# Gated DeltaNet on one core: the last chunk's four heads stacked on the partitions, and 32-row diagonal blocks inverted by substitution without merge products

## The chip, the core and the metric

The kernel runs on one core of a Trainium2 chip. The core has a matrix engine (TensorE, PE in the profile; its weight loads are a row of their own, PEld), a vector engine (DVE), a scalar engine (ACT), GpSimd (POOL), and SyncE (SP), whose queue issues all DMA transfers of this kernel. Each engine has its own instruction stream, and they meet through semaphores. The metric is the device time of one execution in microseconds (us), smaller being better; it is given as the median of several runs.

## The reference, cut

The whole is a decoder trunk of two layers: a gated DeltaNet layer with its MLP, then a differential-attention layer with its MLP, model width 2048, 256 tokens and 16 meta tokens ahead of them, all in float32. The change is in the first layer only. There, for each of 32 value heads (16 heads of queries and keys, each used by two value heads, head width 128), a chunked recurrence is computed:

```python
def step(S, xs):
    qc, kc, vc, bc, gc = xs
    G = jnp.cumsum(gc, axis=-1)
    decay = jnp.exp(jnp.where(tri_incl, G[..., :, None] - G[..., None, :], -jnp.inf))
    kb = kc * bc[..., None]
    a_kk = jnp.where(tri_strict, jnp.einsum('bhik,bhjk->bhij', kb, kc) * decay, 0.0)
    rhs = jnp.concatenate([vc * bc[..., None], kb * jnp.exp(G)[..., None]], axis=-1)
    sol = lax.linalg.triangular_solve(a_kk, rhs, left_side=True, lower=True, unit_diagonal=True)
    u, w = sol[..., :DV], sol[..., DV:]
    v_new = u - jnp.einsum('bhik,bhkv->bhiv', w, S)
    a_qk = jnp.einsum('bhik,bhjk->bhij', qc, kc) * decay
    o = (jnp.einsum('bhik,bhkv->bhiv', qc * jnp.exp(G)[..., None], S)
         + jnp.einsum('bhij,bhjv->bhiv', a_qk, v_new))
    S = (S * jnp.exp(g_last)[..., None]
         + jnp.einsum('bhik,bhiv->bhkv', kc * jnp.exp(g_last - G)[..., None], v_new))
    return S, o
```

What matters is the unit lower triangular system of each chunk and head, and the state `S` that goes from chunk to chunk. Around it stand the input projections (`w_in`: queries, keys, values, an output gate, and the decay and beta logits), a causal convolution of four taps with SiLU, the norms of q and k, and the output projection `w_out`.

## The kernel before, in words

Activations stand with the features on the partitions, 272 tokens in the free dimension. Every large product (`mm3`, lines 147 to 157) runs three times in the type F32R: weights and activations are split into a high part and a rest, and high x high, rest x high and high x rest are summed (lines 152, 155, 156). For this, weights come as 1 MB tiles (`wraw`, three buffers, one DMA each), ACT writes the high part `whi` (line 137), DVE the rest `wlo` (line 139), in halves of 1024 columns. A tile's 16 k-steps are 48 matmuls.

The DeltaNet layer (`gdn`) cuts the 272 tokens into chunks of 128, 128 and 16, and the 32 heads into eight blocks of four. For each block b, in the program's main line: `keys(b)` (four projections for two heads of q and k), `values(b)` (four), `gates(b)` (four), and `gate_out(b - 2)`, the output products of the block before the last (sixteen column tiles of four k-steps). That is 256 k-steps a block. In `gates` and `gate_out` DVE also writes `oT` (line 792) and adds to `acc` (line 1000).

Beside the main line run generators: norms of q and k (`stats`), the score products and decays (`products`), the inverse (`solve`), and the recurrence (`core`). A small planner, `Flow`, decides where their instructions stand in the program. Each k-step of `mm3` advances its clock by 3 x 272 / 2400 = 0.34 units; a generator's `yield x` puts its next piece x units later; `flow.until` runs pieces, with no projection between them, until a condition holds. The scheduler that then orders each engine's instructions need not keep program order: it puts an instruction that is ready ahead of one that is not, and weight splits have high priority.

The steps that the change touches, for a block:

- `stats`: per head and operand, three transposes on PE (`ps_kn`, line 649, one for each chunk) and squares on ACT.
- `products`: per chunk, scores `ps_u` (line 706), decays on ACT (line 710), and `UA` on DVE (line 712), which holds minus the scaled triangle and the query scores. For the first two chunks the diagonal 16-row blocks are copied to DRAM (`scr`, sixteen DMAs, line 718); `below` (POOL) then clears the block diagonal of `UA`. The 16-token chunk is handled head by head on 16 partitions.
- `solve`: all 68 blocks of 16 x 16 (2 chunks x 4 heads x 8, and 4 of the last chunk) are read back as one block per partition (`na`), and `forward` inverts them by substitution, 15 steps of one multiplication (line 630) and one reduction (line 631) each. The inverses go through DRAM into `DT` (block diagonal, 128 x 128 for each chunk and head; lines 751 to 757) and `DT3`. `DT` has one buffer: the next block's solve is written only once the last product that reads it is (`free`).
- `core`: `merge(c)` makes 32-row diagonal inverses from pairs of 16-row ones: a DVE transpose (line 836), a product `ps_e` (line 840), an ACT copy, a product `ps_d` (line 846), an addition and a transpose on DVE (lines 848, 850), then `ps_n` (line 854), from which the chunk's remaining system is applied in three products `ps_a` (line 896) and finished by `ps_w` (line 916). `ps_s` (line 929) updates the state, `ps_o` (line 941) gives the output, `ps_ks` and `ps_qs` (line 880) are the state's part for the next chunk. For the 16-token chunk `ps_w`, `ps_o`, the transposes `ps_ot` (line 810), and the DVE and ACT steps between (lines 884, 947, 951, 966) are issued once for each of the four heads.

A float32 product outside `mm3` is two PE instructions, a transpose one. The planner's waits that the text uses: `SOLVE` 40 units after `solve`, `STEP` 3 units between steps of `core`, 35 and 2 for the last block. The values of block b + 1 (`turned` in `values`) wait for the second chunk of block b (`chunk` = 2), and the main line waits for them by

```python
flow.until(lambda: g["values"] >= hv - 1)
```

Of the kernel before, what the change touches and what calls it, by code (L numbers as in the profile page):

```python
# [21 lines left out]
NM = 16  # L22
SEQ = 256
# [7 lines left out]
G1 = 9  # L31
GB = 4
HOLD = 1
# [469 lines left out]
def gdn(ctx, tc, a, e):  # L503
# [21 lines left out]
    gt = ctx.enter_context(tc.tile_pool(name="gt", bufs=2))  # L525
    gk = ctx.enter_context(tc.tile_pool(name="gk", bufs=4))
# [15 lines left out]
    def decays(ps):  # L542
# [29 lines left out]
        nc.vector.reciprocal(bt, bt)  # L572
        yield GATES[1]
# [10 lines left out]
        nc.sync.dma_start(g_dram, rows)  # L584
        G, GL = gnat[:, 0], gnat[:, 1]
# [5 lines left out]
        nc.scalar.activation(eLast, eLast, AF.Exp)  # L591
        gated.append(True)

    g_dram = dram.tile([32, L], F32, name="g_dram", bufs=1)
# [9 lines left out]
    DT3 = gc.tile([NM, HB, NM], F32, name="DT3")  # L604
    KQ3 = gc.tile([P, 2, 64], F32, name="KQ3")
# [18 lines left out]
    def forward(na, xt):  # L624

        parts, w, n = xt.shape
        tmp = gt.tile([parts, w, n], F32, tag="fw_t", name="fw_t", bufs=1)
        for i in range(1, n):
            b = na[:, None, 0:i + 1, i].broadcast_to([parts, w, i + 1])
            nc.vector.tensor_tensor(tmp[:, :, 0:i + 1], xt[:, :, 0:i + 1], b, ALU.mult)  # L630
            nc.vector.tensor_reduce(xt[:, :, i], tmp[:, :, 0:i + 1], AX.X, ALU.add)
# [4 lines left out]
    def keys(b):  # L636
# [3 lines left out]
        st = gt.tile([P, 2, 3, 2], F32, tag="st", name="st")  # L640
        nc.vector.memset(st, 1.0)
# [3 lines left out]
        def stats(h, t):  # L645
            yield SLACKST
            pk = psk.tile([P, 512], F32, tag="k", name="ps_kn")
            for c, (o, n) in enumerate(CH):
                nc.tensor.transpose(pk[:n, c * P:(c + 1) * P], kq[:, h, t, o:o + n], ident)
            if t == 0:  # L650
                nc.scalar.copy(kn[:, :, h, :], pk[:, :256].rearrange("p (c d) -> p c d", d=P))
            for c, (o, n) in enumerate(CH):
                sq = gt.tile([P, P], F32, tag="dec", name="sqk", bufs=2)
                nc.scalar.activation(sq[:n], pk[:n, c * P:(c + 1) * P], AF.Square, accum_out=st[:n, t, c, h:h + 1])
            if (h, t) == (1, 0):
                yield from products(b, g, st)
# [8 lines left out]
    def products(b, g, st):  # L665
        kq, prev = g["kq"], g["prev"]
        while not gated or prev and not prev["laid"]:
            yield 1.0
        nc.vector.tensor_scalar(st, st, 4 * EPS, None, ALU.add)
        rs = rsqrt(st.rearrange("p t c h -> p (t c h)"), "rsg", [P, 12]).rearrange("p (t c h) -> p t c h", t=2, h=2)  # L670
        rq = g["rq"] = gk.tile([P, 3, 2, 2], F32, tag="sc_rq", name="sc_rq", bufs=2)
        negc = gk.tile([P, 3, 2, 2], F32, tag="sc_nc", name="sc_nc", bufs=2)
        sup = g["sup"] = gk.tile([P, 3, 2, 2], F32, tag="sc_sup", name="sc_sup", bufs=2)
        nk = g["nk"] = gk.tile([P, 3, 2], F32, tag="sc_nk", name="sc_nk", bufs=2)
        r2 = gt.tile([P, 3, 2], F32, tag="r2", name="r2")
        nc.vector.reciprocal(r2, st[:, 0])
        r2b = r2[:, :, :, None].broadcast_to([P, 3, 2, 2])
        nc.vector.tensor_tensor(sup, heads(beta, b), r2b, ALU.mult)
        nc.vector.tensor_scalar(negc, sup, -1.0, None, ALU.mult)

        nc.vector.scalar_tensor_tensor(nk, st[:, 0], 0.5, rs[:, 0], ALU.mult, ALU.mult)
        nc.vector.tensor_tensor(sup, sup, heads(eLast, b), ALU.mult)
        nc.vector.tensor_scalar(rq, rs[:, 1, :, :, None].broadcast_to([P, 3, 2, 2]), P ** -0.5, None, ALU.mult)
# [6 lines left out]
        nc.gpsimd.affine_select(gb[:NM, :, 256:L], gb[:NM, :, 256:L], pattern=[[0, HB], [1, NM]], base=0,  # L690
                                channel_multiplier=-1, compare_op=ALU.is_ge, fill=NEG)
        scr = dram.tile([2, HB, 8, NM, NM], F32, name="scr")
        scr3 = dram.tile([HB, NM, NM], F32, name="scr3")
        UA = g["UA"] = []
        for c, (o, n) in enumerate(CH):
            while prev and prev["chunk"] < min(c, 1):
                yield 1.0
            if c < 2:
                ua = gk.tile([P, HB, 2, P], F32, tag="UA", name="UA", bufs=3)
            else:  # L700
                ua = gk.tile([NM, HB, 2, NM], F32, tag="UA3", name="UA3", bufs=2)
            UA.append(ua)
            for h in range(2):
# [3 lines left out]
                for r in range(2):  # L707
# [4 lines left out]
                    nc.vector.scalar_tensor_tensor(ua[:, hv], pu_v, negc[:n, c, h, r:r + 1],  # L712
                                                   dec[:n, None, :n].broadcast_to([n, 2, n]), ALU.mult, ALU.mult)
                yield UGAP
            if c < 2:
                for bl in range(8):
                    q = slice(NM * bl, NM * bl + NM)
                    nc.sync.dma_start(scr[c, :, bl].rearrange("h j i -> j h i"), ua[q, :, 0, q])
                below(ua, NM)
            else:  # L720
                nc.sync.dma_start(scr3.rearrange("h j i -> j h i"), ua[:, :, 0, :])
# [3 lines left out]
        solve(scr, scr3)  # L725
# [11 lines left out]
    def solve(scr, scr3):  # L737

        nb = 2 * HB * 8
        na = gt.tile([nb + HB, NM, NM], F32, tag="na", name="na", bufs=1)  # L740
        xt = gt.tile([nb + HB, NM, NM], F32, tag="xt", name="xt", bufs=1)
        diag = lambda t: t.rearrange("p j i -> p (j i)")[:, 0:NM * NM:NM + 1]
        nc.gpsimd.memset(xt, 0.0)
        nc.gpsimd.memset(diag(xt), 1.0)
# [4 lines left out]
        scr2 = dram.tile([nb, NM, NM], F32, name="scr2")  # L749
        scr4 = dram.tile([HB, NM, NM], F32, name="scr4")  # L750
        nc.sync.dma_start(scr2, xt[:nb])
        nc.sync.dma_start(scr4, xt[nb:])
        for bl in range(8):
            q = slice(NM * bl, NM * bl + NM)
            nc.sync.dma_start(DT[q, :, :, q].rearrange("p c h j -> p (c h) j"),
                              scr2.rearrange("(x b) m j -> b m x j", b=8)[bl])
        nc.sync.dma_start(DT3, scr4.rearrange("h m j -> m h j"))

    def values(b, g):
# [3 lines left out]
        def turned(hv, vt):  # L763
# [3 lines left out]
            if not nv:  # L767
                nv.extend(gk.tile([P, HB, P], F32, tag="nv", name="nv", bufs=4) for _ in CH)
            pv = psk.tile([P, 512], F32, tag="k", name="ps_v")
            for c, (o, n) in enumerate(CH):  # L770
                nc.tensor.transpose(pv[:n, c * P:(c + 1) * P], vt[:, o:o + n], ident)
            for c, (o, n) in enumerate(CH):
                nc.scalar.activation(nv[c][:n, hv], pv[:n, c * P:(c + 1) * P], AF.Copy,
                                     scale=g["nk"][:n, c, hv // 2:hv // 2 + 1])
            g["values"] += 1

        for hv in range(HB):
# [4 lines left out]
            conv_silu(ps, m, vt)  # L782
            flow.add(turned(hv, vt))
# [11 lines left out]
    def core(b, g):  # L795
# [7 lines left out]
        def turned(c, o, n, ov):  # L803
# [5 lines left out]
            for hv in range(HB):  # L809
                nc.tensor.transpose(pT[:, hv * n:(hv + 1) * n], ov[:n, hv], ident[:n, :n])  # L810
# [9 lines left out]
        ms = gt.tile([P, len(CH), HB], F32, tag="o_ms", name="o_ms")  # L820
# [6 lines left out]
        def merge(c):  # L827

            us = work("us")
            nc.gpsimd.affine_select(us.rearrange("p h (b i) -> p h b i", i=32),  # L830
                                    UA[c][:, :, 0, :].rearrange("p h (b i) -> p h b i", i=32),
                                    pattern=[[0, HB], [-32, 4], [0, 32]], base=0, channel_multiplier=1,
                                    compare_op=ALU.is_ge, fill=0.0)
            below(UA[c], 32)
            e16 = work("e16")
            nc.vector.transpose(flat(e16), flat(DT[:, c]))
            yield step
            _, pE = bank("ps_e")
            for hv in range(HB):
                nc.tensor.matmul(pE[:, hv], us[:, hv], e16[:, hv], start=True, stop=True)  # L840
            ae = work("ae")
            nc.scalar.copy(ae, pE)
            yield step
            _, pD = bank("ps_d")
            for hv in range(HB):
                nc.tensor.matmul(pD[:, hv], ae[:, hv], DT[:, c, hv], start=True, stop=True)
            d32 = work("d32")
            nc.vector.tensor_tensor(d32, DT[:, c], pD, ALU.add)
            dn = work("dn")
            nc.vector.transpose(flat(dn), flat(d32))  # L850
# [6 lines left out]
            merged[c] = d32, NT  # L857
# [5 lines left out]
        for c, (o, n) in enumerate(CH):  # L863
            if c == 0:
                R = nv[0]
            else:
                left = lambda h, t: kq[:, h, t, o:o + n]
                pS, pSv = bank("ps_ks")
                if c < 2:
                    pQ, pQv = bank("ps_qs")  # L870
                    banks = ((pS[:n], 0), (pQ[:n], 1))
                else:

                    nc.scalar.copy(KQ3.rearrange("p h (t i) -> p h t i", i=32)[:, :, :, 0:n], kq[:, :, :, o:o + n])
                    left = lambda h, t: KQ3[:, h, 0:32 + n]
                    banks = ((pS[:32 + n], 0),)
                    pQv = pSv[32:]
# [400 lines left out]
```

## Time and profile before

| | |
|---|---|
| median of 3 runs | 3023.15 us (3022.2 to 3023.69) |
| the profiled execution: its own time | 3024.88 us |
| its span, first to last instruction | 3023.1 us |
| mean granted TensorE clock | 0.993 |
| DeltaNet layer in the span | about 0 to 1045 us |
| DeltaNet blocks with the full load | 125 us each (for example 383 to 508 us) |

The profile is of one execution. Times of windows count from the start of the span. A line of a group reads: source line, engine, operation, output <- inputs by the program's tile names, shapes, count | busy us, mean ns of one | idle time of the engine before them and what ended it. A line of a timeline reads: start, duration, the same name, and in brackets the idle time before and its releaser. Matmuls are pipelined, so their durations overlap, and their starts are to be read. A line of windows reads: window, its length, busy us and count of PE, PEld, DVE, ACT and POOL, granted clock, DMA share, GB/s; by one tile it has only the engine of that tile. A line of waits reads: who waited <- for whom: us in total, times, longest.

### The profile page before, as it was taken

What the parts mean: (1) busy time and instruction counts of PE and PEld (TensorE: products, weight loads), DVE (VectorE), ACT (ScalarE), POOL (GpSimd) and SP (SyncE); (2) the same over time, 40 slices, a digit from 0 to 9 for tenths busy, and PEclk for the clock granted to TensorE, in tenths of its full rate; (3) what the DMA queues carried; (4) which work ended last, traced back from release to release, by engine and by line L of the source; (5) the groups of instructions that cost most, each with busy time, mean ns of one, the idle gap of its engine ahead of it and who ended that gap; (6) DMA issues with size and microseconds to landing.
All of it is one profiled execution on the core that took longest, in us unless ns stands there. A gap on an engine that the chain in (4) does not pass through costs nothing. (4 is left out here: it accounts for less than half of the span.)

```text
span 3023.1 us, 57162 instructions
## 1 busy us (share of the span) xinstructions
PE 2981.0 (99%) x23747; PEld 2924.3 (97%) x23747; DVE 1943.6 (64%) x3452; ACT 1490.1 (49%) x2735; POOL 205.2 (7%) x208
## 2 busy tenths in 40 slices
PE   8999999999999899999999999999999999999998
PEld 8999999999999799999999999999999999999998
DVE  7777576776867674555555558777757555555555
ACT  4565555465555454444344434455555444444443
POOL 0100010000100220000000004300004000000001
PEclk9999999999999899999999999999999999999999
DMA  5433343434434444454544443433354555555553
GB/s 211 151 137 122 142 151 135 156 124 153 146 120 144 153 155 180 168 180 169 179 170 176 173 176 145 153 140 138 143 194 165 184 187 190 183 193 183 191 187 112
DMA packets 92468, 488.36 MB, mean 162 GB/s; under 512 B 29104, under 2 KB 32528, under 8 KB 34736
## 3 DMA queue, kind: packets, MB, share of 16 engines
q1 hardware_dynamic: 92208, 484.70, 44.6%
q8 instruction: 187, 3.06, 0.4%
q14 instruction: 73, 0.60, 0.1%
HBM read 481.41 MB, written 3.25 MB: 160 GB/s over the span
## 5 line engine op out<-in xcount | busy, mean ns | idle before, releaser
L139 DVE TENSOR_TENSOR wlo<-wraw,whi 128x1024 fp32r<-128x1024 f32 x872 | 1070.0, 1229 | 770.8 <-ACT whi L137 769.5
L137 ACT ACTIVATE whi<-wraw 128x1024 fp32r<-128x1024 f32 x890 | 940.2, 1059 | 1145.7 <-PE ps_dn L156 432.1
L152 PE MATMUL ps_dn<-yh,whi 128*128 128x272 f32 (+1 forms) x2048 | 583.2, 285 | 0.0
L152 PE MATMUL ps_up<-xh,whi 128*128 128x272 f32 (+1 forms) x2048 | 582.8, 285 | 0.0
L156 PE MATMUL ps_dn<-yl,whi 128*128 128x272 f32 (+1 forms) x2048 | 582.3, 284 | 0.0
L155 PE MATMUL ps_up<-xh,wlo 128*128 128x272 f32 (+1 forms) x2048 | 581.0, 285 | 0.2 <-DVE wlo L139 0.2
L155 PE MATMUL ps_dn<-yh,wlo 128*128 128x272 f32 (+1 forms) x2048 | 580.9, 284 | 0.0
L156 PE MATMUL ps_up<-xl,whi 128*128 128x272 f32 (+1 forms) x2048 | 580.3, 285 | 0.1
L152 PE MATMUL ps_in<-xh,whi 128*128 128x272 f32 x1520 | 460.2, 303 | 0.0
L156 PE MATMUL ps_in<-xl,whi 128*128 128x272 f32 x1520 | 441.6, 291 | 0.8 <-DVE xl L320 0.8
L155 PE MATMUL ps_in<-xh,wlo 128*128 128x272 f32 x1520 | 441.3, 291 | 0.0
L152 PEld LDWEIGHTS ps_up<-xh,whi 128*128 128x128 f32 x2048 | 385.9, 188 | 0.5 <-ACT xh L401 0.4
L155 PEld LDWEIGHTS ps_dn<-yh,wlo 128*128 128x128 f32 x2048 | 386.0, 188 | 0.0
L152 PEld LDWEIGHTS ps_dn<-yh,whi 128*128 128x128 f32 x2048 | 385.5, 188 | 0.0
L156 PEld LDWEIGHTS ps_up<-xl,whi 128*128 128x128 f32 x2048 | 384.8, 188 | 0.5 <-DVE xl L409 0.5
L155 PEld LDWEIGHTS ps_up<-xh,wlo 128*128 128x128 f32 x2048 | 384.6, 188 | 0.5 <-DVE wlo L139 0.5
L156 PEld LDWEIGHTS ps_dn<-yl,whi 128*128 128x128 f32 x2048 | 384.8, 188 | 0.0
L152 PEld LDWEIGHTS ps_in<-xh,whi 128*128 128x128 f32 x1520 | 287.2, 189 | 7.7 <-issue 4.9
L155 PEld LDWEIGHTS ps_in<-xh,wlo 128*128 128x128 f32 x1520 | 287.6, 189 | 1.6 <-issue 0.4
L156 PEld LDWEIGHTS ps_in<-xl,whi 128*128 128x128 f32 x1520 | 286.6, 189 | 1.4 <-DVE xl L320 1.0
L475 DVE TENSOR_TENSOR acc<-acc,ps_dn 128x272 f32<-128x272 f32 (+1 forms) x224 | 95.9, 428 | 122.1 <-PE ps_dn L156 121.4
L152 PE MATMUL ps_at<-xh,whi 128*128 128x272 f32 x512 | 154.5, 302 | 0.0
(313 smaller groups left out, 4476.9 us busy)
## 6 DMA issues: line engine op xcount, KB each, us to landing
wraw<-w_up SPq DMA_DIRECT2D x128, 1024.0 KB, 4.8
wraw<-w_down SPq DMA_DIRECT2D x128, 1024.0 KB, 4.8
wraw<-w_in SPq DMA_DIRECT2D x97, 1024.0 KB, 4.8
wraw<-w_out SPq DMA_DIRECT2D x32, 1024.0 KB, 4.9
wraw<-w_kv SPq DMA_DIRECT2D x32, 1024.0 KB, 4.8
wraw<-w_q SPq DMA_DIRECT2D x16, 1024.0 KB, 5.8
wraw<-w_o SPq DMA_DIRECT2D x16, 1024.0 KB, 5.6
gb<-g_dram SPq DMA_DIRECT2D x8, 544.0 KB, 5.6
```

What stands on the lines that cost most here:

```text
L137: nc.scalar.activation(hi, part, AF.Copy)
L139: inst = eng.tensor_tensor(lo, part, hi.bitcast(F32), ALU.subtract)
L152: one = nc.tensor.matmul(ps, wh, rh, start=(k == 0), stop=False)
L155: nc.tensor.matmul(ps, wl, rh, start=False, stop=False)
L156: ring["mm"] = nc.tensor.matmul(ps, wh, rl, start=False, stop=(k == nk - 1))
L475: nc.vector.tensor_tensor(acc[:, m, :N], acc[:, m, :N], ps[:, :N], ALU.add)
```

## The change

- Blocks of 32 rows: the 32 diagonal blocks of the first two chunks are stored (eight DMAs), loaded to four groups of 32 partitions, and each group computes a quarter of the inverse's columns (every fourth). `forward` has 31 steps; step i works on the first min(8, i // 4 + 1) columns of a group and i + 1 rows. It became a generator that lets the planner advance 3 units after every eighth step.
- `merge` keeps the DVE transpose, now of `DT` itself, and `ps_n`; the products `ps_e` and `ps_d` with their copies, additions and selections are gone.
- The 16-token chunk has the four heads on 64 partitions: keys and queries of the four heads are copied side by side (`kc`), one transpose and one score product serve all, masks make the triangle block diagonal, `forward` runs a second time with 64 partitions (one column each, 15 steps), `DT3` is a 64 x 64 block diagonal, `ps_w`, `ps_o` and the transpose are one instruction group each. `ps_ks` becomes four accumulated products over shifted windows of a zero-padded `KQ3`. Per-row factors in this layout (`G3`, `beta3`) are made once, with thirteen more DMAs, in `decays`.
- The work pool `g1` has seven buffers for nine.

```diff
@@ decays
+        nc.sync.dma_start(b_dram, bt[:NM, 2, :])
 ...
+        for h in range(HB):
+            nc.sync.dma_start(beta3[NM * h:NM * h + NM], by_head(b_dram)[h])
+            for t in range(2):
+                q = TQ * t + NM * h
+                nc.sync.dma_start(G3[q:q + NM], g_dram[:, 256:L].rearrange("(b h) i -> h i b", h=HB)[h])
@@ forward
-    def forward(na, xt):
+    def forward(na, xt, w, per, name):
 ...
         for i in range(1, n):
-            b = na[:, None, 0:i + 1, i].broadcast_to([parts, w, i + 1])
-            nc.vector.tensor_tensor(tmp[:, :, 0:i + 1], xt[:, :, 0:i + 1], b, ALU.mult)
-            nc.vector.tensor_reduce(xt[:, :, i], tmp[:, :, 0:i + 1], AX.X, ALU.add)
+            k = min(w, i // per + 1)
+            b = na[:, None, 0:i + 1, i].broadcast_to([parts, k, i + 1])
+            nc.vector.tensor_tensor(tmp[:, :k, 0:i + 1], xt[:, :k, 0:i + 1], b, ALU.mult)
+            nc.vector.tensor_reduce(xt[:, :k, i], tmp[:, :k, 0:i + 1], AX.X, ALU.add)
+            if i % RUN == RUN - 1:
+                yield RUNGAP
@@ stats
-            for c, (o, n) in enumerate(CH):
+            for c, (o, n) in enumerate(LATE):
                 nc.tensor.transpose(pk[:n, c * P:(c + 1) * P], kq[:, h, t, o:o + n], ident)
@@ products
+        for t in range(2):
+            nc.scalar.copy(kc[:, t].rearrange("p (h r) i -> p h r i", r=2),
+                           kq[:, :, t, 256:L][:, :, None, :].broadcast_to([P, 2, 2, NM]))
 ...
+        nc.tensor.transpose(pk[:, :P], kc, ident)
 ...
+                nc.tensor.matmul(pu[:TQ, :P], kc[:, :TQ], kc, start=True, stop=True)
+                dec = gt.tile([P, P], F32, tag="dec", name="dec", bufs=2)[:TQ, :TQ]
+                nc.scalar.activation(dec.rearrange("p (h i) -> p h i", i=NM), gb3, AF.Exp, bias=G3[:TQ, b:b + 1])
+                nc.vector.scalar_tensor_tensor(ua, pu[:TQ, :P].rearrange("p (t i) -> p t i", t=2), negc[:TQ, 8:9],
+                                               dec[:, None, :].broadcast_to([TQ, 2, TQ]), ALU.mult, ALU.mult)
 ...
-        solve(scr, scr3)
+        yield from solve(scr, scr3)
@@ solve
-        nc.sync.dma_start(na[:nb], scr.rearrange("c h b j i -> (c h b) j i"))
-        nc.sync.dma_start(na[nb:], scr3)
-        nc.vector.memset(diag(na), 1.0)
-        forward(na, xt)
+        for r in range(4):
+            nc.scalar.copy(flat(xt)[:, r:r + (NS + 4) * (NS // 4 - 1) + 1:NS + 4], e4[:, r:r + 1].broadcast_to([P, NS // 4]))
+        nc.scalar.copy(xs[:, 0], eye_s)
+        blocks = scr.rearrange("c h b j i -> (c h b) (j i)")
+        nc.sync.dma_start(flat(na), blocks[None, :, :].broadcast_to([4, P // 4, NS * NS]))
+        nc.sync.dma_start(flat(ns), scr3.rearrange("h j i -> h (j i)")[:, None, :].broadcast_to([HB, NM, NM * NM]))
 ...
+        yield from forward(na, xt, NS // 4, 4, "fw_t")
+        scr2 = dram.tile([P // 4, NS, NS], F32, name="scr2")
+        for q, cols in enumerate(scr2.rearrange("x (s q) j -> q x s j", q=4)):
+            nc.sync.dma_start(cols, xt[P // 4 * q:P // 4 * (q + 1)])
+        yield from forward(ns, xs, 1, NM, "fw_s")
+        nc.sync.dma_start(scr4, xs[:, 0])
 ...
@@ values
+            if hv == HB - 1:
+                nc.tensor.transpose(pv[:TQ, 256:384], g["vc"].rearrange("p h i -> p (h i)"), ident)
+                nc.scalar.activation(nv[2], pv[:TQ, 256:384], AF.Copy, scale=g["nk"][:TQ, 4:5])
 ...
+            nc.scalar.copy(g["vc"][:, hv], vt[:, 256:L])
@@ core, merge
-            us = work("us")
-            nc.gpsimd.affine_select(us.rearrange("p h (b i) -> p h b i", i=32), ...
-            below(UA[c], 32)
-            e16 = work("e16")
-            nc.vector.transpose(flat(e16), flat(DT[:, c]))
-            yield step
-            _, pE = bank("ps_e")
-            for hv in range(HB):
-                nc.tensor.matmul(pE[:, hv], us[:, hv], e16[:, hv], start=True, stop=True)
-            ae = work("ae")
-            nc.scalar.copy(ae, pE)
-            yield step
-            _, pD = bank("ps_d")
-            for hv in range(HB):
-                nc.tensor.matmul(pD[:, hv], ae[:, hv], DT[:, c, hv], start=True, stop=True)
-            d32 = work("d32")
-            nc.vector.tensor_tensor(d32, DT[:, c], pD, ALU.add)
             dn = work("dn")
-            nc.vector.transpose(flat(dn), flat(d32))
+            nc.vector.transpose(flat(dn), flat(DT[:, c]))
             yield step
             _, pN = bank("ps_n")
@@ core, last chunk
+                pS, _ = bank("ps_ks")
+                for hv in range(HB):
+                    w0 = TQ - NM - NM * hv
+                    nc.tensor.matmul(pS[:, :P], KQ3[:, hv // 2, w0:w0 + P], S[:, hv, :], start=(hv == 0), stop=(hv == HB - 1))
+                few = lambda name: gt.tile([P, 1, P], F32, tag="g3", name=name, bufs=3)
+                R = few("R3")
+                nc.vector.scalar_tensor_tensor(R[:TQ, 0], pS[:TQ, :P], neG3[:TQ, b:b + 1], nv[2], ALU.mult, ALU.add)
+                ov = few("ov3")
+                nc.scalar.copy(ov[TQ:, 0], pS[TQ:, :P])
+                yield step
+                pw, _ = bank("ps_w")
+                nc.tensor.matmul(pw[:TQ, :P], DT3, R[:TQ, 0], start=True, stop=True)
+                g["free"] = True
+                w = few("w3")
+                nc.scalar.copy(w[:TQ, 0], pw[:TQ, :P])
+                yield step
+                po, _ = bank("ps_o")
+                nc.tensor.matmul(po[:, :P], UA[2].rearrange("p t i -> p (t i)"), w[:TQ, 0], start=True, stop=True)
 ...
```

More of the change, by code (lines that the diff above doesn't have):

```diff
@@ L22 @@
 NM = 16
+NS = 32
+NBL = P // NS
+RUN, RUNGAP = 8, 3.0
 SEQ = 256
@@ L30 @@
 LAG = 2
-G1 = 9
+G1 = 7
 GB = 4
+TQ = HB * NM
 HOLD = 1
@@ L603, in gdn @@
     nc.vector.memset(DT, 0.0)
-    DT3 = gc.tile([NM, HB, NM], F32, name="DT3")
-    KQ3 = gc.tile([P, 2, 64], F32, name="KQ3")
+    DT3 = gc.tile([TQ, TQ], F32, name="DT3")
+    nc.vector.memset(DT3, 0.0)
+    eye_s = gc.tile([HB * NM, NM], F32, name="eye_s")
+    e4 = gc.tile([P, 4], F32, name="e4")
+    nc.vector.tensor_reduce(e4, ident.rearrange("p (q x) -> p q x", q=4), AX.X, ALU.add)
+    nc.vector.tensor_reduce(eye_s, ident[:HB * NM, :HB * NM].rearrange("p (h j) -> p j h", j=NM), AX.X, ALU.add)
+    KQ3 = gc.tile([P, 2, 2 * TQ + TQ - NM], F32, name="KQ3")
     nc.vector.memset(KQ3, 0.0)
@@ L675, in products @@
[L675 to L683, printed above, removed]
+        kc = gk.tile([P, 2, HB, NM], F32, tag="kc", name="kc", bufs=1)
@@ L697, in products @@
                 yield 1.0
[L698 to L701, printed above, removed]
+            if c == 2:
+                ua = gk.tile([TQ, 2, TQ], F32, tag="UA3", name="UA3", bufs=2)
+                UA.append(ua)
+                pu = psk.tile([P, 512], F32, tag="k", name="ps_u")
+                nc.tensor.matmul(pu[:TQ, :P], kc[:, :TQ], kc, start=True, stop=True)
[3 more added lines that the diff above has]
+                                               dec[:, None, :].broadcast_to([TQ, 2, TQ]), ALU.mult, ALU.mult)
+                yield UGAP
+                for h in range(HB):
+                    q = slice(NM * h, NM * h + NM)
+                    nc.sync.dma_start(scr3[h], ua[q, 0, q])
+                break
+            ua = gk.tile([P, HB, 2, P], F32, tag="UA", name="UA", bufs=3)
             UA.append(ua)
@@ L748, in solve @@
-        forward(na, xt)
[L749 to L754, printed above, removed]
+        na = gt.tile([P, NS, NS], F32, tag="na", name="na", bufs=1)
+        ns = gt.tile([HB * NM, NM, NM], F32, tag="ns", name="ns", bufs=1)
+        xt = gt.tile([P, NS // 4, NS], F32, tag="xt", name="xt", bufs=1)
@@ L759, in values @@
+        for h in range(HB):
+            q = slice(NM * h, NM * h + NM)
+            nc.sync.dma_start(DT3[q, q], scr4[q])
     def values(b, g):
@@ L819, in core @@
         outs = []
-        ms = gt.tile([P, len(CH), HB], F32, tag="o_ms", name="o_ms")
+        ms = gt.tile([P, 9], F32, tag="o_ms", name="o_ms")
         nc.vector.memset(ms, 1.0)
@@ L910, in core @@
                 nc.vector.tensor_tensor(z, z, p3, ALU.add)
-            else:
-                z, dt = R, DT3
-            yield step
-            _, pw = bank("ps_w")
-            for hv in range(HB):
-                nc.tensor.matmul(pw[:n, hv], dt[:, hv, :], z[:n, hv], start=True, stop=True)
-            if c == 2:
-                g["free"] = True
-            if c < 2:
+                yield step
+                _, pw = bank("ps_w")
+                for hv in range(HB):
+                    nc.tensor.matmul(pw[:n, hv], dt[:, hv, :], z[:n, hv], start=True, stop=True)
                 ws = work("ws")
```

182 lines of the change are left out of this document (103 added, 79 removed).

## The prediction

> **What bounds the kernel now.** I read the page first, then the time by stage, then who waits for whom in the first third of the span, where the edited code runs, then PE's timeline there.
>
> ```profile
> span 3023.1 us, 57162 instructions
> PE 2981.0 (99%) x23747; PEld 2924.3 (97%) x23747; DVE 1943.6 (64%) x3452; ACT 1490.1 (49%) x2735; POOL 205.2 (7%) x208
> ...
> 383.00:508.00 125.00, 125.00 (x984) 121.63 (x984) 90.52 (x192) 69.55 (x167) 8.48 (x10) 1.00 0.40 142
> ...
> ACT whi L137 <- PE ps_in L156: 176.9, 112, 3.1
> DVE wlo L139 <- ACT whi L137: 175.3, 144, 5.0
> PE ps_kn L649 <- DVE kq L622: 1.9, 1, 1.9
> ```
>
> PE is busy 99%, and in the window of one block of four heads (383 to 508 us; the columns are PE, weight loads, DVE, ACT, POOL) it never stops, while DVE works 90.5 of 125 us. The waits from 60 to 1002 us say it more strictly: PE's one wait of weight there is of 1.9 us. ACT waits for PE to free weight buffers and DVE for ACT, so the weight split follows PE. An instruction taken off PE is therefore time, until DVE or the end of the stage decides. The price comes from PE's timeline (start, duration, group):
>
> ```profile
> 460.97 1.05 PE L840 MATMUL ps_e<-e,us 128*128 128x128 f32 x8
> 461.78 0.37 PE L152 MATMUL ps_in<-xh,whi 128*128 128x272 f32 x1
> 461.99 0.29 PE L155 MATMUL ps_in<-xh,wlo 128*128 128x272 f32 x1
> 462.12 0.29 PE L156 MATMUL ps_in<-xl,whi 128*128 128x272 f32 x1
> ...
> 407.82 0.29 PE L156 MATMUL ps_in<-xl,whi 128*128 128x272 f32 x1
> 408.04 1.04 PE L916 MATMUL ps_w<-R,DT 16*16 16x128 f32 x8
> 409.02 0.40 PE L152 MATMUL ps_in<-xh,whi 128*128 128x272 f32 x1
> ...
> 412.94 1.04 PE L941 MATMUL ps_o<-w,UA 16*16 16x128 f32 x8
> ...
> 403.82 1.06 PE L880 MATMUL ps_ks<-S,KQ 128*48 128x256 f32 x4
> ...
> 435.36 0.42 PE L810 MATMUL ps_ot<-ident,ov 16*128 16x16 f32 x4
> ...
> 382.06 0.49 PE L649 MATMUL ps_kn<-ident,kq 128*128 128x128 f32 x3
> 382.39 0.60 PE L706 MATMUL ps_u<-kq 128*128 128x256 f32 x2
> ```
>
> Durations overlap, starts do not. The projection's matmuls start 0.13 us apart (461.99 to 462.12). The eight `ps_e` instructions (four heads, two per f32 product) push the next projection from 460.97 to 461.78, and the one after it comes 0.21 instead of 0.13 later: 0.81 + 0.08 = 0.89 us.
>
> **The change part by part.** *Merge products.* `ps_e` and `ps_d` go, in two chunks of eight blocks: 4 x 0.89 = 3.6 us a block, 28.5 us in all. `ps_n` stays.
>
> *Last chunk.* Against a start 0.13 after the last projection, the same reading gives `ps_w` 409.02 - 407.95 + 0.1 = 1.17 us; `ps_o` has the same shape, count and duration, 1.17; `ps_ks`, 0.02 longer, about 1.2; the four `ps_ot`, 0.42 long, about 0.5. `ps_w` and `ps_o` become one 64-row product of two instructions each. No row shows that shape. Two instructions at 0.11 give 0.22; the eight 16-row ones cost 0.28 more than eight full ones, so 0.22 + 0.28 = 0.50 is the other end. I take 0.40, nearer the small shape: 0.77 saved twice. `ps_ks` becomes eight full instructions, 0.89: 0.3 saved. One `ps_ot` for four: 0.2. The third transpose of each `ps_kn` and `ps_v` (0.11, a third of 382.06 to 382.39) goes eight times and two new transposes come: about 0.5. Two small `ps_u` pairs become one product: 0.3. Together 2.8 us a block, 22.5 in all (20 to 25 by the ends). PE loses **51 us**, 48 to 54.
>
> *Substitution on DVE.* Rows of the window 380 to 510 (count, busy, mean ns):
>
> ```profile
> L630 DVE TENSOR_TENSOR fw_t<-xt,na 68x256 f32<-68x256 f32 x1 | 0.6, 618 | 0.0
> L630 DVE TENSOR_TENSOR fw_t<-xt,na 68x64 f32<-68x64 f32 x1 | 0.3, 259 | 0.0
> L631 DVE TENSOR_REDUCE xt<-fw_t 68x16 f32<-68x256 f32 x1 | 0.4, 421 | 0.0
> L631 DVE TENSOR_REDUCE xt<-fw_t 68x16 f32<-68x64 f32 x1 | 0.2, 206 | 0.0
> L836 DVE STREAM_TRANSPOSE e<-DT 128x512 f32<-128x512 f32 x2 | 1.4, 705 | 0.0
> L848 DVE TENSOR_TENSOR d<-DT,ps_d 128x512 f32<-128x512 f32 x2 | 1.4, 685 | 0.1
> L884 DVE SCALAR_TENSOR_TENSOR R<-ps_ks,neG,nv 16x128 f32<-16x128 f32 x4 | 1.2, 332 | 1.2 <-PE ps_ks L880 1.2
> ...
> 383.00:508.00 125.00, 11.29 (x30) 1.00 0.40 142
> ...
> 417.00:427.00 10.00, 10.00 (x82) 9.98 (x81) 9.93 (x30) 6.20 (x17) 0.00 (x0) 1.00 0.52 192
> 427.00:437.00 10.00, 10.00 (x82) 9.82 (x82) 6.05 (x10) 6.48 (x16) 2.82 (x4) 1.00 0.48 139
> ```
>
> A multiply costs 139 ns + 1.87 per element, a reduction 134 + 1.12. The new loop has 31 steps over min(8, i//4 + 1) x (i + 1) elements, 3047 in sum: 31 x 273 ns + 3047 x 2.99 ns = 17.6 us; the 16-step one for the stacked chunk (135 elements) 4.5. So 22.1 us instead of 11.3 (the window by that tile). Gone are two transposes and two additions (2.8), three of four `R` (1.0), as many `ov` of its kind (1.0) and some of `UA` (0.6). DVE gains 5.4 us a block: 96 of what becomes 118.6 us, 81%. That fits on average. Locally it is tight: from 417 to 427 DVE is already full (9.93 of 10). After 427 it has about 4 us in ten free, so 11 more us are worked off in some 25 to 30 us, by about 457, while the weight split takes its turns between the dependent steps, as it does now. I cost this at 3 us over blocks 1 to 7 (0 to 25: the upper end is a wait as in block 0, below, in every block).
>
> The strided read is a choice: column i of `na` is read 64 B apart now, 128 B after. The Trainium skill (SBUF — State Buffer, § Door 1: The DMA port swizzle) says an access pays whenever it leaves its 16-byte line, which both strides do each time; by it 1.87 ns stays. The trace agrees as far as its 1.87 stands against 1.12 for the packed reduction; its doubling with the stride would add 5.7 us a block, DVE 86%, and move chance to the first rival below.
>
> Block 0 has no matrix chain to let the split run ahead, and there PE did wait:
>
> ```profile
> 121.29 0.55 PE L649 MATMUL ps_kn<-ident,kq 128*128 128x128 f32 x3 [1.86 <-DVE kq L622]
> ...
> 121.30:125.00 3.70, 3.70 (x21) 3.68 (x22) 2.91 (x5) 2.12 (x8) 1.70 (x3) 0.66 0.34 123
> ```
>
> PE stood 1.86 us, and the granted clock then fell to 0.66 over the next 3.7 us, about 1.3 more: 3.2 us. A longer loop at that place costs me 3 us (0 to 8). The Trainium skill (TensorE: Matmul & The Clock Gate, § Part 1: The HAM clock gate (the "warmup" mystery)) has windows of 3.4 us at half clock after an idle one; here a gap shorter than a window sufficed. By the Trainium skill such a wait would cost its 1.9 alone, by the row 3.2.
>
> *The planner.* A block's projections advance its clock by 256 x 0.34 = 87 units. Per block the chain now waits 40 + 12 (merge) + 15 + 18 + 3 = 88 units before the next solve may be written; after, 18 + 40 + 6 + 15 + 18 + 3 = 100. So the main loop runs into `flow.until` about 13 units each block, and chain steps are written back to back. The trace shows what that does, in block 1, where 44 units are skipped already because blocks 0 and 1 carry no output products:
>
> ```profile
> 273.52 1.16 PE L896 MATMUL ps_a<-t,NT 128*128 128x128 f32 x8
> 275.45 1.16 PE L896 MATMUL ps_a<-z,NT 128*128 128x128 f32 x8
> ...
> 504.38 1.05 PE L896 MATMUL ps_a<-R,NT 128*128 128x128 f32 x8
> 509.87 1.05 PE L896 MATMUL ps_a<-t,NT 128*128 128x128 f32 x8
> ...
> SPq L751 <- DVE xt L631: 26.6, 7, 4.5
> 429.60 4.52 SPq L755 DMA_DIRECT2D DT<-scr  x8
> 439.31 0.71 DVE L836 STREAM_TRANSPOSE e<-DT 128x512 f32<-128x512 f32 x1
> ```
>
> Steps follow 1.9 us apart instead of 5.5, later projections fill between, and PE has no wait: I cost it at nothing. The cover is the projections the scheduler can pull forward; without it 13 units are some 14 us a block. The inverse is not late either: now `DT` is stored from 429.6 and transposed at 439.3, 21 us before PE uses it (460.97); the loop ends some 25 us later, its use moves 18 units.
>
> *Queues.* SP issues 27 small DMAs a block instead of 30 (about 0.55 us each, 4.52 / 8), so queue time falls. Its stores still wait for the loop (4.5 us at most), with weight loads queued behind; three raw buffers cover that. Thirteen DMAs are new, once, in the gates: 7 us of SP near 70 us; 1 us (0 to 3). POOL loses the two selections of each merge; nobody waits on POOL. ACT gains eleven small copies a block and loses the `ae` copies and most four-fold steps of the last chunk, so it does not rise.
>
> *End of the stage.* The last block's chain runs out of projections:
>
> ```profile
> 1003.24 1.06 PE L880 MATMUL ps_ks<-S,KQ 128*48 128x256 f32 x4
> 1018.11 1.16 PE L810 MATMUL ps_ot<-ident,ov 16*128 16x16 f32 x4 [5.48 <-ACT ov L966]
> 1020.09 0.60 PE L152 MATMUL ps_out<-oh,whi 128*128 128x272 f32 x1 [0.83 <-ACT oh L979]
> ```
>
> Those 16.9 us shrink to about 10, as four-fold steps on DVE, ACT and PE become single. But the chain starts 18 - 4 = 14 units later, so about four more steps at 2.2 us lie bare: +9 - 7 = **+2** (-6 to +10).
>
> **Sum.** -51 + 3 + 3 + 1 + 2 = -42 us. The profiled execution took 3024.88 us (span 3023.1); 2983 after. The median of the runs is 1.7 lower, so **2981**.
>
> **Rivals.** *DVE becomes the bound.* The full stretch starves the split and PE waits in every block, 3.2 us as at 121 or twice that: 8 x 3.2 to 8 x 6.4 = 26 to 51 on -51 + 3 (the end and the gates), so 3001 to 3026 by the median, mostly near 3005. For: DVE full at 417 to 427, twice the loop, the wait at 121. Against: the slack after 427.
>
> *The planner's 13 units turn into PE waits* (the slower side): if the pulled-forward projections run out, 14 us x 7 = 98 against -51, about 3070. It decides against the change from 51 / 7 = 7.3 us of wait a block. For: stacked projections hold PSUM banks until the chain frees their buffers. Against: block 1.
>
> *Nothing gained:* the freed PE time turns into waits for weights, 3023. Against: the split waits for PE, not PE for it.
>
> **Chances.** Forecast 0.64 (its own range 2965 to 2997), DVE 0.20, planner 0.10, nothing 0.06. The range 2963 to 3014 leaves out the planner, part of the third and the fast edge. 0.2% (6 us) is about what a measurement here can tell from none: faster 0.82, same 0.08, slower 0.10.
>
> **What would show it.** Right: no `ps_e` and `ps_d`, blocks 118 to 120 us apart, PE's waits from 60 to 1002 us under 15 us in sum, the two loops near 22 us a block, a bare end of 15 to 22 us. Wrong: PE waits on `wlo` or `kq` behind the loop, clock below 1.00 in blocks 2 to 6, multiplies well over 139 ns + 1.87 an element, or `DT` landing after PE wants it.

## The result and the profile after

The changed kernel takes 3058.9 us (median; 3057.4 to 3060.3), the kernel before 3023.4 measured beside it: ratio 1.0118, interval 1.010 to 1.0135. It is **35.5 us slower**, where 2981 was forecast. The page of the profiled execution, totals and busy times:

```profile
span 3056.4 us, 56602 instructions
PE 2961.9 (97%) x23339; PEld 2910.6 (95%) x23339; DVE 1971.0 (64%) x3865; ACT 1459.0 (48%) x2640; POOL 175.3 (6%) x176
```

PE did lose work: 408 instructions and 19 us. But its share fell from 99 to 97%: it now stands. DVE's and PE's waits from 60 to 1080 us (who waited for whom: sum, times, longest), which cover the DeltaNet stage:

```profile
DVE na L804 <- DMA na<-scr: 34.4, 5, 9.2
DVE cv_a L643 <- issue: 21.3, 3, 8.3
...
PE ps_ks L937 <- DVE S L997: 24.2, 5, 6.8
PE ps_w L981 <- DVE z L977: 15.5, 4, 7.7
PE ps_in L159 <- DVE wlo L143: 5.6, 1, 5.6
```

Before, neither DVE row was in the list, and PE's longest wait up to 1002 us was 1.9 us. One block's timeline, first SP's queue, then DVE, then the PE product that waited:

```profile
399.39 0.57 SPq L802 DMA_DIRECT2D na<-scr  x1
400.00 0.47 SPq L124 DMA_DIRECT2D wraw<-w_in  x1
...
403.76 0.43 DVE L647 SCALAR_TENSOR_TENSOR vt<-ps_in,cv_a 128x272 f32<-128x272 f32 x1
410.72 0.09 DVE L804 MEMSET na<- 128x32 f32 x1 [6.53 <-DMA na<-scr]
...
413.54 0.17 DVE L657 TENSOR_REDUCE xt<-fw_t 128x2 f32<-128x16 f32 x1
413.62 1.22 DVE L143 TENSOR_TENSOR wlo<-wraw,whi 128x1024 fp32r<-128x1024 f32 x1
414.76 1.12 DVE L997 SCALAR_TENSOR_TENSOR S<-S,eGL,ps_s 128x128 f32<-128x128 f32 x4
...
416.02 2.05 PE L937 MATMUL ps_ks<-S,KQ 128*128 128x128 f32 x8 [6.20 <-DVE S L997]
```

`na` was issued at 399.39, and its memset, the first DVE instruction of the substitution, started 11.3 us later. While it waited, DVE ran nothing of what stood behind it. Behind the memset stood seven steps of the loop, a weight split and then `S`, whose data had long been there; behind `S`, PE. The same moment by engine (PE, weight loads, DVE, ACT, POOL busy, granted clock, DMA share, GB/s):

```profile
406.00:410.00 4.00, 3.82 (x28) 3.50 (x27) 0.00 (x0) 1.65 (x3) 0.00 (x0) 1.00 0.30 90
410.00:416.00 6.00, 0.00 (x0) 0.01 (x1) 4.73 (x21) 0.00 (x0) 0.00 (x0) 0.74 0.24 60
416.00:420.00 4.00, 3.98 (x18) 3.87 (x18) 2.80 (x20) 1.50 (x7) 0.00 (x0) 0.54 0.60 238
```

Six us without a matmul, then four at about half clock. PE has such a gap in each of the eight blocks, 3.5 to 7.7 us, and there are 64.9 us of half clock ahead of the first `ps_up` instead of 20.5. In five blocks the trace names the load as what DVE waited for. In the other three it names nothing (`issue`), and the instruction `cv_a` starts 0.02 us ahead of the memset; but in all eight the memset starts 0.7 to 1.3 us after the load's last packet.

The eight gaps are 47.4 us in sum, and half clock went on for 35.8 us behind them, in which the projections' matmuls start 0.227 us apart instead of 0.127. By an estimate from these numbers the stalls cost 47.4 + 35.8 x 0.44 = 63 us.

The first `ps_up`, where the DeltaNet stage is over, comes at 1077.1 us instead of 1053.0. That is 24.1 of the 33.3 us by which the spans differ. The other 9.1 arise after it, in code that the change doesn't touch: from the first `ps_up` to the end 1979.2 us instead of 1970.1. So there are two losses to explain.

### The profile page after: what moved, and what is told of

Same layout as the page of the kernel before. It is cut to its first block, busy times and chain, and to the rows that moved or that the text cites. A ratio compares the mean times of both kernels' runs of the same rounds, so it can differ in the third digit from the quotient of the medians.

```text
span 3056.4 us, 56602 instructions
## 1 busy us (share of the span) xinstructions
PE 2961.9 (97%) x23339; PEld 2910.6 (95%) x23339; DVE 1971.0 (64%) x3865; ACT 1459.0 (48%) x2640; POOL 175.3 (6%) x176
```

## Experiments

Theory A: the load of `na`, 512 KB by one broadcast, comes late, and the memset at the head of DVE's queue turns that into standing. Theory B: the loop itself overloads DVE. Theory C: the planner's added units delay the chain.

**The load in four parts.**

```diff
-        nc.sync.dma_start(flat(na), blocks[None, :, :].broadcast_to([4, P // 4, NS * NS]))
+        for q in range(4):
+            nc.sync.dma_start(flat(na)[P // 4 * q:P // 4 * (q + 1)], blocks)
```

> The changed kernel with na loaded by four transfers of 32 partitions x 4 KB each instead of one broadcast of four times 32 rows; everything else stays. Theory A (the load of na, 11 us in the changed kernel, holds VectorE in its in-order queue at the memset of na, the chain and then PE stand 5 to 8 us a block, and each gap is followed by 3.4 to 10 us of half clock): na lands within 6 us, the memset waits under 2 us, half clock before the end of the DeltaNet stage falls from 65 to some 20 to 30 us, and the time is 2980 to 3000 us. Theory B (the substitution itself overloads VectorE): the waits stay in sum, 3045 to 3060. Theory C (the planner's 12 units more per block push the chain late): no change, 3055 to 3062.

2993.7 us, ratio 0.9904 (0.9890 to 0.9919) to the kernel before: one line is worth 65 us against the changed kernel's 3058.9. The `na` rows of that kernel, and one block by engine, then DVE's two loops in the same block:

```profile
L805 DVE MEMSET na<- x8: 85/85/85, 107.9 to 862.5; 128x32 f32 x8
its engine sat idle before it (us, times) until:
who waited for it (us, times):
  ACT xs L800: 2.2, 2
...
DMA to landing us min/median/max: 2.2/2.7/3.1
...
498.90:618.50 119.60, 118.98 (x927) 116.50 (x926) 93.42 (x243) 65.10 (x152) 3.92 (x7) 1.00 0.45 155
...
498.90:618.50 119.60, 18.36 (x62) 1.00 0.45 155
...
498.90:618.50 119.60, 4.49 (x30) 1.00 0.45 155
```

The same bytes, 2.7 us to land, no wait at `na`, and the clock at 1.00. The first `ps_up` comes 63.6 us earlier than in the changed kernel, about what the stalls were estimated to cost. The loop and the planner's units are as they were, so B and C would have kept the stalls. Half clock ahead of the first `ps_up`: 13.7 us.

**Why one transfer is slow.** The same 128 packets of 4 KB as two broadcasts of two (`for q in range(2): ... broadcast_to([2, P // 4, NS * NS])`):

> The changed kernel with na by two broadcast loads of two times 32 rows instead of one of four times 32. The same 128 packets of 4 KB in the same bytes. One load of leading dimension 4 took 7.3 to 11 us for them, four loads of leading dimension 32 took 2.2 to 3.2. If the leading dimension sets over how many DMA engines a load is spread: two loads over two engines each, 9 us where they fall on different engines and 16 to 20 where on the same; time 3055 to 3130. If what counts is into how many transfers it is cut: some 5 us and 3000 to 3030.

3081.6 us (one execution). From the first packet to the last the load took 13.4 to 16.8 us, against 7.3 to 11.0 with one broadcast of four. So the number of transfers is not what made the load slow. A window with nothing else going on, with one row ahead of it from DVE's timeline:

```profile
424.01 0.09 DVE L805 MEMSET na<- 128x32 f32 x1 [11.77 <-DMA na<-scr]
...
418.00:423.00 5.00, 0.00 (x0) 0.00 (x0) 0.00 (x0) 0.00 (x0) 0.00 (x0) 0.88 0.13 50
```

A DMA share of 0.13 is two of sixteen engines. The packets say the same: in this load of block 3, 128 packets of 0.21 us in 13.5 us are 2.0 at work at a time; in the changed kernel, 128 of 0.28 us in 9.2 us are 3.9; in the four-load kernel 12.6. The Trainium skill (DMA: Bandwidth & Descriptors, § Rules for kernel authors) says just that: an outermost dimension of c < 16, "a leading zero-stride broadcast of c copies" among its examples, confines a transfer to at most c engines. The trace agrees for c = 4 and c = 2. Two transfers with two packets at work between them also mean that both pairs fell on the same two engines.

**The place in the queue.** Three kernels moved the wait instead of the load. The first lets ten planner units pass ahead of the memset (`yield NAGAP`, 10.0):

> The changed kernel with ten planner units (10 us of projections) between the issue of na's load and the memset of na with which VectorE begins; the load itself stays slow. A: the memset finds its data, no stall of 5 to 8 us is left; the chain starts up to 10 us later in each block, which costs nothing in the middle and up to 10 us in the last block: 2985 to 3010. B: the loop takes as long as before and the stalls move with it: 3045 to 3065. C: ten more units in each block make it slower than the changed kernel by 10 us or more: over 3065.

3066.1 us, ratio 1.0145 (1.013 to 1.016). That is C's range (over 3065), though 7 us above the changed kernel and not 10. But the change of place did not happen: the chains moved some 8 us later, the load with them, and the schedule put the memset right behind `z` again, as the waits show:

```profile
DVE na L806 <- DMA na<-scr: 59.5, 8, 8.7
```

So units of the planner did not keep the memset from the head of DVE's queue, and this run decides nothing about A. In the four-load kernel the schedule had put the memset behind `R3` in four blocks, so two more kernels parted place and duration. Slow load, memset bound behind the previous block's `R3` (`in_order(first, prev["r3"])`):

> The changed kernel with its one slow broadcast load of na, and one thing added: from block 1 on, the memset of na is bound on VectorE to come after R3, the last chunk's right-hand side of the block before. In the changed kernel it stands ahead of S, ov and R3 in seven blocks; in the four-load kernel the order that the schedule gave has it behind R3 in blocks 2 to 5, so that its gain could come from the order and not from the load. If the place in VectorE's queue is what turns the slow load into lost time: the load still takes 7 to 11 us, but S no longer stands behind it, and the time falls to 2993 to 3010. If the slow load costs time wherever the memset stands (its packets hold up other loads, or DT lands too late): 3040 to 3060.

3046.4 us, ratio 1.008 (1.0063 to 1.0097): the second range by the number, with 12.5 us back. But another load took over the part, as this kernel's waits show:

```profile
DVE ns L808 <- DMA ns<-scr: 36.9, 7, 8.7
DVE na L805 <- DMA na<-scr: 9.4, 2, 7.8
```

`ns` is a broadcast of leading dimension 4 as well, issued behind `na`, and its memset was not bound. What the place alone is worth stays open. The converse, a fast load with its memset at high priority:

> The four-load kernel with the memset of na at high priority, so that in blocks 2 to 5 it stands ahead of the last S, ov and R3 on VectorE again. If the fast load is enough by itself, no wait at na and 2990 to 2997. If it needed the place behind R3 as well: waits of 2 us and more at na, 3005 to 3030.

2997.5 us (one execution) and no wait at `na`. The priority did less than was meant: in blocks 3 to 5 the memset came ahead of `ov` and `R3` but not of `S`, and in block 2 of none of them. Blocks 6 and 7 of the four-load kernel answer the question instead. There the memset stands 3.9 us ahead of `S`, as it stood 4.0 us ahead in blocks 3 to 5 of the changed kernel. It starts 3.4 to 3.6 us after the load's last packet, with no wait. At the same place in the queue, a fast load is enough.

**The wait alone, in the kernel before.** Two broadcasts of 256 KB into a tile that is free then, and a memset that waits for them:

```diff
 ...
+        for k in range(2):
+            nc.sync.dma_start(far[:, 512 * k:512 * k + 512], rows[None, :, :].broadcast_to([4, 32, 512]))
+        nc.vector.memset(far[:, 0:1024:512], 1.0)
         nc.vector.memset(diag(na), 1.0)
```

> The kernel before, with nothing of the change, plus two broadcast loads of 256 KB (4 times 32 rows of 2 KB each) from the same scratch beside na's, and one VectorE memset of 2 elements a row that waits for them ahead of the substitution; what is loaded is not used. It adds the suspected wait alone. A: VectorE stands 5 to 10 us at that memset in each block, PE stands behind it and loses clock: 3060 to 3100. B and C: neither the loop nor the planner changed, so 3021 to 3028.

3038.2 us, ratio 1.0052 (1.0035 to 1.0069). The direction is A's, the size is not: 15 us, where 37 to 77 were expected. The last of the data came 5.6 to 7.9 us after the first packet, sooner than the changed kernel's 7.3 to 11.0, and DVE stood less:

```profile
DVE far L751 <- DMA far<-scr: 13.2, 7, 4.6
```

13 us of standing on DVE, 15 us of time. B and C had no change here.

**The 9 us behind the stage.** One-column tiles of the reciprocal root are new, and move all later tiles up by 192 bytes. The kernel before with only an unused tile of 192 bytes, then of 256 (`npool.tile([P, 24], ...)` and `[P, 32]`, two buffers each):

> The kernel before with one unused tile of 2 x 96 bytes a partition in the pool of small tiles; no instruction is added or taken. All tiles of the later stages that are allocated after it move up by 192 bytes, as they do in the changed kernel (its one-column reciprocal root has tiles of its own there). From the first product of ps_up to the end the kernel before takes 1970.1 us, the changed kernel 1979.2, and the two variants of it so far 1978.0 and 1978.8, while the variant of the kernel before takes 1968.5. Theory T (the places of the tiles make the matmuls of the later stages longer, 119 ns instead of 117.5 in the second MLP): this stretch 1977 to 1980 and the time 3030 to 3033. Rival (the stretch is longer for another reason, such as what the DeltaNet stage leaves behind): 1969 to 1971 and 3022 to 3025.

> The kernel before with an unused tile of 2 x 128 bytes a partition in the pool of small tiles, so that the later tiles lie 256 bytes higher (192 bytes higher gave 1977.1 us instead of 1970.1 from the first ps_up to the end). If any other place costs the same: 1976 to 1979. If the distance counts modulo 128 or 256 bytes: 1969 to 1972.

3030.5 us, ratio 1.0023 (1.0014 to 1.0032), with 192; 3024.5 (one execution) with 256, as before. From the first `ps_up` to the end: 1977.1 and 1970.2. In the second MLP, 400 us of nothing but matmuls, in this order before, changed, 192 and 256 bytes:

```profile
2400.00:2800.00 400.00, 400.00 (x3411) 400.00 (x3411) 226.44 (x274) 176.49 (x221) 0.00 (x0) 1.00 0.52 187
...
2427.00:2827.00 400.00, 400.00 (x3382) 400.00 (x3382) 224.60 (x272) 175.03 (x218) 0.00 (x0) 1.00 0.52 185
...
2400.00:2800.00 400.00, 400.00 (x3382) 400.00 (x3381) 225.16 (x273) 174.69 (x219) 0.00 (x0) 1.00 0.51 185
...
2400.00:2800.00 400.00, 400.00 (x3411) 400.00 (x3410) 226.63 (x275) 176.52 (x220) 0.00 (x0) 1.00 0.52 187
```

3411 or 3382 matmuls: 117.3 or 118.3 ns each, at full clock. No instruction differs between the first, third and fourth row; only where the tiles lie does. Put back in the four-load kernel (the one-column root in the first column of the four-column tiles):

> The changed kernel with the four loads of na (2993.7 us) and with the one-column reciprocal root in the first column of the four-column tiles, so that the pool of small tiles has its size of before and the later tiles their places of before. T: the stretch from the first ps_up to the end falls to 1969 to 1971 us, and the time to 2984 to 2987. Rival: 2992 to 2995.

2988.4 us, ratio 0.9887 (0.9874 to 0.9901), with 3411 again. It is just outside the theory's range, and behind the first `ps_up` it takes 1972.3 us, where 1969 to 1971 were expected. So the tiles account for 7 of the 9 us. The other 2 lie in the attention layer, between the first `ps_at` and the first `ps_sc` (122.9 us, 120.6 before), and their cause stays open.

**Each half alone.** The first kernel has the stacked last chunk alone: the changed kernel with `NS = 16` and `G1 = 9`, and with the substitution, `ps_e` and `ps_d` of the kernel before (its tiles also lie 192 bytes higher). The second has the 32-row blocks alone: the kernel before with `NS = 32`, `G1 = 7` and the `solve` of the four-load kernel, without `ps_e` and `ps_d`, the last chunk by head.

> The half of the change that stacks the last chunk's heads, alone: the 16-row blocks, their substitution and the merge products ps_e and ps_d are those of the kernel before (na is 64 KB again; the small blocks of the last chunk have their own 15 steps behind it). The prediction's term for this half is 2.8 us less of PE a block, 22.5 in all. A: no wait at na, 2995 to 3008. If the stacking is worth little (its products run beside other work anyway, or the small loop costs what it saves): 3015 to 3025. If its waits are what cost the time: over 3030.

> The other half of the change alone: 32-row blocks by substitution without ps_e and ps_d, na by four loads, the small blocks of the last chunk as in the changed kernel, but the last chunk's products by head as before. Tiles of the later stages lie where they lay before. By the prediction's term (ps_e and ps_d are 28.5 us of PE) 2993 to 3000. If the two halves only pay together, since the stacking alone gave the DeltaNet stage 12 us more instead of 22 less: by the difference to the four-load kernel (39.5 us less up to the first ps_up) this half would give some 50 us and the time were 2970 to 2978.

3041.4 us, ratio 1.0061 (1.0046 to 1.0076), and 3003.2, ratio 0.9936 (0.9922 to 0.9949). The first lies in its third range (its waits cost the time), the second is 3 us above its forecast, and that the halves only pay together (2970 to 2978) did not come. Up to the first `ps_up` the blocks alone give 19.0 us and both halves together 39.5, but the stacking alone costs 12 us (and its tiles 7 more behind the stage). Its products did get 19 us cheaper on PE by group, start to start. Small PE waits ate that: PE is 11.6 us less busy from 60 to 320 us, and the stretch from the last projection to the first `ps_up` grew by 11. The first of these windows is of the kernel before, the second of the stacking alone:

```profile
60.00:320.00 260.00, 257.92 (x1984) 247.51 (x1984) 194.69 (x439) 150.09 (x376) 23.69 (x32) 0.99 0.40 139
...
60.00:320.00 260.00, 246.36 (x1877) 236.63 (x1876) 198.59 (x513) 139.91 (x342) 24.93 (x36) 0.99 0.39 135
```

Why these waits appear in the one mix and not in the other stays open.

**The end, the planner and DVE's reserve**, on the four-load kernel with its tiles put back: `STEP7 = (2.0, 5.0, 17.0)`; then `SOLVE = 22.0` as well; then the loop run twice.

> The changed kernel with the four loads and the tiles at their places of before (2988.4 us), and with 17 instead of 35 planner units between the last block's solve and its chain: the solve itself takes 18 units since the change, so the chain is laid out again at the distance that it had from the solve's beginning in the kernel before. In the four-load kernels PE runs out of products of ps_out some 25 us before the last block's chain ends. If that chain begins too late: 10 to 17 us less, 2971 to 2979. If its data set the beginning (DT landing, the loop on VectorE) or the same work is only moved: 2985 to 2990.

> As end_17, and in the other seven blocks too the units between solve and chain go from 40 to 22. Theory A says that the planner's units cost nothing in the middle, since PE has projections to run meanwhile: as end_17 within 3 us. Theory C (the chain is 18 units late in each block and PE pays for it): 8 us or more below end_17. If the chain now comes before DT has landed: PE waits at ps_n and 10 us or more above end_17.

> The changed kernel with the four loads and the tiles at their places of before (2988.4 us), with the 31 steps of the substitution run a second time on their own result, so that the result isn't the reference's: some 17 us more of VectorE in each block, which takes it from 78 to about 90 per cent of the DeltaNet stage, and 12 planner units more. Theory A (VectorE was never the bound, only its queue was blocked by a load): 2985 to 3000. Theory B (VectorE is at its limit with one loop): the most part of 8 x 17 us comes on top, 3050 to 3120.

2982.6, ratio **0.9861** (0.9845 to 0.9878), the fastest of all; 2991.6, ratio 0.9890 (0.9876 to 0.9905); and 3105.6 (one execution). The end gave 5.7 us and not 10 to 17. Starting the middle chains earlier cost 9 us and gained none, so the units were no loss there; by what the 9 us come is open. With the loop twice, 18 us of DVE work more a block, the last projection comes only 35 us later, but the last chain product 120: each chain lags further behind, until PE has nothing else, with its longest wait, of 30.2 us, in the last block:

```profile
PE ps_n L908 <- DVE dn L904: 39.0, 4, 30.2
```

So B's range came true for two loops, and A's failed. For one loop, B is refuted by the four-load kernel. What sets the limit with two is not shown. From block 2 on, the loops of successive blocks begin 127 to 132 us apart, where the projections of a block took 120, but DVE is busy in only 81% of the time from 60 to 1000 us. It can be DVE's turns between dependent steps, or the length of a block's chain, which has 12 planner units more as well.

## Why the prediction was wrong

The step that failed is *Queues*, with *Substitution on DVE* beside it. It counted SP's DMAs (27 for 30) and asked whether weight loads would be late behind them. It gave no term to the load of `na`, which had grown from 64 to 512 KB and changed its form, and it didn't ask what stands behind the DVE instruction that waits for it. That priced a wait at zero which costs 65 us. Of the signs named for being wrong, the clock below 1.00 in blocks 2 to 6 appeared, but from the load and not from the loop. PE waited on `wlo` only once, in block 0 (5.6 us); elsewhere it waited on `S` and `z`, which stood behind the memset. The planner rival's 3070 lies nearest to 3058.9, and that is chance: the four-load kernel keeps the planner's units and has no such gap.

The second miss, 7 us, was in no step either: the memory that a helper takes for a new shape moved the tiles of later stages.

What held, read in the four-load kernel:
- *Sum:* -42 predicted, -39.5 up to the first `ps_up`: -42.0 up to the last projection (for -44) and +2.5 behind it. The time is 2993.7 for 2981, and 2988.4 with the tiles put back. Blocks in the middle lie 119.8 to 120.2 us apart (124.7 to 125.2 before), at the upper end of the 118 to 120 forecast.
- *Merge products:* `ps_e` and `ps_d` held 27.3 us of PE, start to start, for 28.5. *Last chunk:* about 20 for 22.5, by the same reading.
- *Loop:* 18.4 + 4.5 = 22.9 us a block for 22.1; DVE 93.4 of 119.6, 78%, for 81%. The multiply cost 1.85 ns an element from 64 to 256 elements, for 1.87 before: it didn't double with the stride.
- *Planner* at nothing: so in the middle. *Block 0:* its 3 us were not needed; with the fast load PE has no gap there.
- *End of the stage:* last projection to last chain product 57.2 us for 55.8 before: +1.4 for +2. But the part without output products, read as the prediction's 16.9 us were, is 28.7 us (950.9 to 979.6), where 15 to 22 were forecast. The claim that `DT` and its use are not late was not what failed.
- Rival *DVE becomes the bound:* not with one loop. A second one costs 117 us, so the kernel is nearer to some limit than the 78% makes it look.

## What to carry to other kernels

When a change makes a load bigger or turns it into a broadcast, cost it as an operation: its bytes, its outermost dimension, when it lands, and what stands in the queue behind the instruction that waits for it. Put a large dimension outermost (here 32 rows), or cut the transfer so. And after a change of tile sizes compare a stretch that was not edited: if its matmuls per 400 us differ, pad the pool back before judging the change.

## What the hardware showed unexpectedly

- From its first packet to its last, a 512 KB load took 2.2 to 3.2 us as four transfers with 32 rows outermost, 7.3 to 11.0 as one with 4, and 13.4 to 16.8 as two with 2.
- 192 bytes of offset made F32R matmuls of 256 columns take 118.3 instead of 117.3 ns at the same granted clock; 256 bytes did nothing. Which of the operands' places counts was not tried.
- PE gaps of 3.5 to 7.7 us each brought 3.4 to 10.2 us of half clock, which began 2.6 to 5.2 us after PE had stopped. The 2.8 to 6.0 us of it that lay behind the gap cost time on top of the gap.
